# Hybrid decoder block: the residual's 128x128 transposes move from TensorE to VectorE blocks and SBUF-to-SBUF DMAs

## The chip, the cores and the metric

The kernel runs on one core of one Trainium2 chip. The metric is the device time of one execution in microseconds, the median of three runs. One execution was also taken by the hardware profiler; its trace is what the views below are read from.

## The reference, cut to what matters

The reference is one layer of a decoder: three head groups read one normed input, their outputs are joined and projected, a residual is added, and cross-attention into a memory follows. All is float32, 256 tokens, width 2048. The change touches the path from the first residual to the cross-attention's queries:

```python
y = concatenate([y_lru, y_ml, y_mo], axis=-1)     # (256, 2048)
x = x + y @ w_out[l]                              # the residual x1
hx = rms_norm(x, xa_norm_g[l])
hm = rms_norm(mem, mem_norm_g[l])
x = x + memory_cross_attention(hx, hm, xa_wq[l], xa_wkv[l], xa_wo[l])
return rms_norm(x, final_norm_g)
```

In memory_cross_attention the queries are `hx @ wq`, a product over the 2048 channels, so x1, which `y @ w_out` leaves with tokens on the partitions, is wanted with channels on the partitions.

## The kernel before, in words

**Weights.** All weight matrices are one stream of 172 chunks of up to 512 KB, taken in a fixed order of groups (GROUPS). For chunk i, `load(i)` issues one DMA on SP (L172) into one of 4 buffers `raw`; `split(i)` makes a rounded half on ScalarE (L197, `wh`) and the rest on VectorE (L148, `wl`), 6 buffers each; `mm(i)` multiplies on TensorE (L260 and L261 for groups with channels out, L282 to L284 for groups with tokens out). Activations are split in the same way into pairs of tiles (`a_x`, `a_y`, `a_m`, `a_h`).

**The loop.** One step of the main loop traces, in this order: the split of chunk i+4 and the load of chunk i+8; `mm(i)`; the work that a group's last chunk starts (`done`); and one call of `step()`. The order is written out by hand: every engine and SP's queue runs its instructions in the order in which the loop traces them. `step()` advances the first generator in a queue to its next yield; when a generator is at its end, the same call goes on with the next one. `urgent` puts a generator at the head of the queue, `bg` at its tail. `load(i+8)` waits until `split(i+4)` has freed its `raw` buffer, and `split(i+4)` until `mm(i-2)` has freed its `wh` and `wl`.

**The groups around the change.** out0 to out3 are the four quarters of `y @ w_out`, 8 chunks each; ck0 and ck2 (4 chunks each) make the memory's keys from `a_m`; cq0 and cq2 (4 each) make the queries from `a_h`; cv follows. In each step of out3 `stage_split("m", j)` also makes one pair `a_m`: two ScalarE (L232) and two VectorE instructions (L151). `a_m` j takes the buffer of `a_y` j, so it waits until out3's matmuls of step j have read that.

**The residual.** At the end of out group g, `x1_evac(a, g)` goes to the head of the queue. Its first part adds the accumulators to x (VectorE, two of 128x512) and sums squares on ScalarE, through a scratch tile `yt` of one buffer (L852). Its next two parts, one a step, each do four 128x128 transposes on TensorE into PSUM (L858) and split the result into a pair `a_h` (`split_pair`: L239 on ScalarE, L148 on VectorE). So x1_evac holds the head of the queue for the step of the group's end and two more; in the step after those it ends and the next generator goes on.

**Behind it in the queue** wait x1_load(2) and x1_load(3) (DMAs of x, L843), then mem_stats: eight steps that load a piece of the memory (L222), each squared two steps later on ScalarE (into `yt`) and summed on GpSimd (L402), two idle steps, and `stats("m")`: four tiny matmuls (L426) on the sum of the squares, a power on GpSimd (L359), two VectorE instructions that write a diagonal tile into `yt` (L430), and one step later a matmul that reads that `yt` (L433).

A tile that is asked for again (one buffer, same tag) waits until everything that was traced on the old one has run, also what was traced later. Tag w1 holds the memory's keys from ck0's end, w2 the queries from cq0's end; both are free from out0's end until then.

Of the kernel before, what the change touches and what calls it, by code (L numbers as in the profile page):

```python
# [105 lines left out]
def kernel(ctx: ExitStack, tc: tile.TileContext, xT, memT, x, mem, ws, vec_d, lw_d, fg_d, out):  # L106
    nc = tc.nc
    V, S, P, G = nc.vector, nc.scalar, nc.tensor, nc.gpsimd
# [18 lines left out]
    def ps():  # L127
        nps[0] += 1
        return psp.tile([128, 512], F32, tag="ps", name=f"ps{nps[0]}")

    def big(tag, *shape):
        n = 1
        for s in shape:
            n *= s
        t = wk.tile([128, 1556], F32, tag=f"w{tag}", name=f"w{tag}")
        v = t[:, :n]
        if len(shape) == 2:
            v = v.rearrange("p (a b) -> p a b", a=shape[0])
        elif len(shape) == 3:
            v = v.rearrange("p (a b c) -> p a b c", a=shape[0], b=shape[1])  # L140
        return v

    def small(name, *shape):
        t = sm.tile([128, *shape], F32, name=name, tag=name)
        return t

    def tt(out, a, b, op):
        V.tensor_tensor(out, a, b, op)  # L148
# [58 lines left out]
    def act_pair(which, j):  # L207

        a = acts.tile([128, 2, 2, 256], F32R, tag="y" if which in "ym" else "x", name=f"a_{which}{j}")
        act_all[which][j] = a  # L210
        act_hi[which][j], act_lo[which][j] = a[:, :, 0, :], a[:, :, 1, :]
        return act_hi[which][j], act_lo[which][j]
# [22 lines left out]
    def split_pair(which, j, src):  # L235

        h, l = act_pair(which, j)
        src = src.rearrange("p (a b) -> p a b", a=2)
        S.activation(h, src, AF.Copy)  # L239
        tt(l, src, h.bitcast(F32), OP.subtract)  # L240
# [70 lines left out]
    p = ps()  # L311
    for _ in range(WARM):
        P.matmul(p[:, :256], ones[:, :128], ones, start=True, stop=True)
    ident = cst.tile([128, 128], F32, name="ident")
# [522 lines left out]
    X1 = {}  # L837
# [9 lines left out]
    def x1_evac(a, g):  # L847
        t1 = X1[g]
        for t in range(2):
            tt(t1[:, t, :], a[t], t1[:, t, :], OP.add)  # L850
            junk = small("yt", 512)
            S.activation(junk, t1[:, t, :], AF.Square, accum_out=ssq1[:, t, g:g + 1])  # L852
        yield
        for j in range(2):
            p = ps()
            for kk in range(2):
                for t in range(2):
                    P.transpose(p[:, kk * 256 + t * 128:kk * 256 + t * 128 + 128],  # L858
                                t1[:, t, (2 * j + kk) * 128:(2 * j + kk) * 128 + 128], ident)
            split_pair("h", 2 * g + j, p)  # L860
            yield

    def x1_rstd():
# [130 lines left out]


    queue = deque()

    def bg(*gens):
        queue.extend(gens)
# [6 lines left out]

    def step(n=1):

        while queue and n > 0:
            try:  # L1010
                if next(queue[0]):
                    return
                n -= 1
            except StopIteration:
                queue.popleft()

    def drain():
        while queue:
            step()

    def idle(n):
# [18 lines left out]
    def done(name, a):  # L1040
# [17 lines left out]
        elif name[0] == "q":  # L1058
            urgent(qk_evac("q", 7, a, int(name[1])))
        elif name[0] == "k":  # L1060
            urgent(qk_evac("k", 5, a, int(name[1])))
            if name == "k2":
                bg(ml_norm())
        elif name == "v0":
            urgent(v_evac(a, 0))
        elif name == "v1":
            urgent(v_evac(a, 1))
            bg(mo_heads())
        elif name == "z0":
            urgent(gate_z(name, a))  # L1070
        elif name == "z1":
            urgent(gate_z(name, a))
            bg(ml_y(), mo_y(0, 1))
        elif name == "z2":
            urgent(gate_z(name, a))
            bg(mo_y(1, 3), x1_load(0), x1_load(1), x1_load(2), x1_load(3), mem_stats())
        elif name.startswith("out"):
            g = int(name[3])
            urgent(x1_evac(a, g))
            if g == 3:  # L1080
                bg(x1_rstd())
        elif name.startswith("ck"):
            urgent(ck_evac(a, int(name[2])))
        elif name.startswith("cq"):
            urgent(cq_evac(a, int(name[2])))
        elif name == "cv":
            C["acc"] = a
# [12 lines left out]
    for i in range(NS):  # L1100
        while nsx < 8 and nsx <= i + 2:
            stage_split("x", "mix_g", nsx)
            nsx += 1
        while nsp <= min(i + SPLIT_AHEAD, max(i + 2, 2 * i - 2)):
            split(nsp)
            nsp += 1
            while nl < nsp + RAW_BUFS:
                load(nl)
                nl += 1
        mm(i)  # L1110
        if i == 0:
            late_consts()
        if 2 <= i < 6:
            xrow_load(i - 2)
        if i == 6:
            nc.sync.dma_start(lw, lw_d)
        if 6 <= i < 10:
            xrow_square(i - 6)
        g, j, kc = CHUNKS[i][:3]
        if GROUPS[g][0] == "out3":  # L1120
            stage_split("m", "mem_g", j)
        if (j + 1) * kc == NK:
            done(GROUPS[g][0], acc.pop(g))
        step()
    drain()
    cv_out(C["acc"])
    fg_load((1, 9))
# [67 lines left out]
```

## Time and profile before

| | us |
|---|---|
| median of 3 runs (521.16 to 522.33) | 522.2 |
| the profiled execution | 521.88 |
| its span, first to last instruction | 520.2 |
| TensorE busy (98% of the span) | 507.9 |
| VectorE busy (65%) | 338.0 |
| ScalarE busy (56%) | 292.8 |
| GpSimd busy (11%) | 54.8 |

The profiled execution's time and its span differ by 1.7 us, which lie outside the profiled instructions. PE is TensorE, PEld its weight loads, DVE VectorE, ACT ScalarE, POOL GpSimd, SP SyncE; SPq is SP's queue, which issues the DMAs. Matmuls are pipelined: one that is 0.39 us long may be followed by the next after 0.23 us, so what a matmul takes of the path is the distance from start to start. The granted clock was 1.00 in all stretches from 318 to 482 us.

### The profile page before, as it was taken

To read this page: it belongs to the slowest core of one execution; us is meant where nothing else is said; L and a number is where in the kernel's file an instruction comes from. 1 tells how busy PE (TensorE), PEld (TensorE's weight loads), DVE (VectorE), ACT (ScalarE), POOL (GpSimd) and SP (SyncE) were. 2 spreads that over 40 slices of the span, in tenths; PEclk is the share of its full clock that TensorE was granted. 3 is DMA by queue.
4 is the path that set the end of the run, shared out by engine and by line. 5 is a ranking of instruction groups with operands and counts; after the bars stand their busy time and mean duration, and the time that the engine had idled before them with its cause. 6 is when DMAs were issued, how large, how long until landed. Compare 5 with 4: busy or idle time off the path is not lost.

```text
span 520.2 us, 7578 instructions
## 1 busy us (share of the span) xinstructions
PE 507.9 (98%) x2814; PEld 448.8 (86%) x2814; DVE 338.0 (65%) x531; ACT 292.8 (56%) x476; POOL 54.8 (11%) x70
## 2 busy tenths in 40 slices
PE   8999999999999999999999999999999999999993
PEld 6999889998988888889988888888888888888883
DVE  5958848895397656548645466654658749637574
ACT  5775477678544333353545755543649467546353
POOL 2800001000132100002000000000132003000000
PEclk9999999999999999999999999999999999999998
DMA  8995635467446544435843465478575527734704
GB/s 274 360 412 180 187 120 167 139 221 230 160 160 178 186 161 163 151 92 183 271 155 121 137 209 179 164 272 325 188 264 174 194 66 259 237 128 129 234 3 161
DMA packets 31077, 98.74 MB, mean 190 GB/s; under 512 B 3520, under 2 KB 3904, under 8 KB 31040
## 3 DMA queue, kind: packets, MB, share of 16 engines
q1 hardware_dynamic: 30896, 98.25, 56.9%
q8 instruction: 22, 0.36, 0.3%
q14 instruction: 15, 0.12, 0.1%
q10 hardware_dynamic: 144, 0.01, 0.0%
HBM read 96.15 MB, written 2.10 MB: 189 GB/s over the span
## 4 chain that ended last, share of the span: by engine, by line
PE 85%; issue 6%; POOL 3%; DVE 3%; DMA 1%; ACT 1%; SPq 1%; POOLq 0%; ACTq 0%; DVEq 0%
PE acc_out L284 5%; PE acc_out L282 5%; PE acc_out L283 5%; PE acc_q L260 4%; PE acc_k L260 4%; PE acc_z L284 4%; PE acc_z L282 4%; PE acc_z L283 4%; PE acc_cq L260 3%; PE acc_lz L260 3%; PE acc_q L261 2%; PE acc_k L261 2%; PE acc_o L283 2%; PE acc_o L282 2%; PE acc_o L284 2%
## 5 line engine op out<-in xcount | busy, mean ns | idle before, releaser
L148 DVE TENSOR_TENSOR wl<-raw,wh 128x1024 fp32r<-128x1024 f32 (+3 forms) x166 | 199.6, 1212 | 111.7 <-ACT wh L197 109.3
L197 ACT ACTIVATE wh<-raw 128x1024 fp32r<-128x1024 f32 (+2 forms) x162 | 161.8, 1013 | 44.5 <-DMA raw<-ws 14.8
L282 PE MATMUL acc_out<-wh,a_y 128*128 128x512 f32 x128 | 50.8, 397 | 0.0
L284 PE MATMUL acc_out<-wh,a_y 128*128 128x512 f32 x128 | 49.9, 390 | 0.0
L283 PE MATMUL acc_out<-wl,a_y 128*128 128x512 f32 x128 | 49.8, 389 | 0.0
L282 PE MATMUL acc_z<-wh,a_x 128*128 128x512 f32 x96 | 39.6, 412 | 0.0
L284 PE MATMUL acc_z<-wh,a_x 128*128 128x512 f32 x96 | 37.6, 391 | 0.0
L283 PE MATMUL acc_z<-wl,a_x 128*128 128x512 f32 x96 | 37.5, 390 | 0.0
L260 PE MATMUL acc_k<-a_x,wh 128*128 128x512 f32 x96 | 34.4, 401 | 0.0
L260 PE MATMUL acc_q<-a_x,wh 128*128 128x512 f32 x96 | 34.1, 398 | 0.0
L451 POOL TENSOR_TENSOR w<-ev,rrow 128x512 f32<-128x512 f32 x11 | 17.5, 1589 | 153.6 <-DVE ev L148 153.6
L284 PEld LDWEIGHTS acc_out<-wh,a_y 128*128 128x128 f32 x128 | 24.0, 188 | 5.2
L283 PEld LDWEIGHTS acc_out<-wl,a_y 128*128 128x128 f32 x128 | 24.1, 188 | 4.7
L282 PEld LDWEIGHTS acc_out<-wh,a_y 128*128 128x128 f32 x128 | 24.1, 188 | 4.6
L261 PE MATMUL acc_k<-a_x,wl 128*128 128x256 f32 x96 | 26.9, 280 | 0.0
L261 PE MATMUL acc_q<-a_x,wl 128*128 128x256 f32 x96 | 26.8, 280 | 0.0
L402 POOL TENSOR_TENSOR mask<-mask,yt 128x512 f32<-128x512 f32 x7 | 10.3, 1473 | 147.1 <-ACT yt L401 147.1
L260 PE MATMUL acc_lz<-a_x,wh 128*128 128x512 f32 x64 | 23.3, 406 | 0.0
L260 PE MATMUL acc_ck<-a_m,wh 128*128 128x512 f32 x64 | 23.1, 403 | 0.0
L260 PE MATMUL acc_cq<-a_h,wh 128*128 128x512 f32 x64 | 22.7, 399 | 0.0
L283 PE MATMUL acc_o<-wl,a_x 128*128 128x392 f32 (+1 forms) x64 | 21.6, 338 | 0.0
L282 PE MATMUL acc_o<-wh,a_x 128*128 128x392 f32 (+1 forms) x64 | 21.6, 337 | 0.0
(302 smaller groups left out, 1187.4 us busy)
## 6 DMA issues: line engine op xcount, KB each, us to landing
raw<-ws SPq DMA_DIRECT2D x138, 512.0 KB, 4.1
raw<-ws SPq DMA_DIRECT2D x24, 384.0 KB, 3.1
w<-x SPq DMA_DIRECT2D x8, 512.0 KB, 6.5
raw<-ws SPq DMA_DIRECT2D x8, 392.0 KB, 3.1
w<-memT SPq DMA_DIRECT2D x8, 256.0 KB, 6.1
out<-xg SPq DMA_DIRECT2D x8, 256.0 KB, 3.0
w<-xT SPq DMA_DIRECT2D x7, 256.0 KB, 6.7
raw<-ws SPq DMA_DIRECT2D x4, 256.0 KB, 5.0
```

What stands on the lines that cost most here:

```text
L148: V.tensor_tensor(out, a, b, op)
L197: S.activation(h[:, :kc * n], r[:, :kc * n], AF.Copy)
L260: P.matmul(a[m], h[:, sl], both, start=first, stop=False, skip_group_check=True)
L261: P.matmul(a[m][:, :256], l[:, sl], xh, start=False, stop=last, skip_group_check=True)
L282: P.matmul(o, xh[:, sl], mh, start=first, stop=False)
L283: P.matmul(o, xh[:, sl], ml, start=False, stop=False)
L284: P.matmul(o, xl[:, sl], mh, start=False, stop=last)
L402: G.tensor_tensor(sq[which], sq[which], q, OP.add)
L451: G.tensor_tensor(dst, e, rb(which), OP.mult)
```

## The change: what it does, and the diff

x1_evac ends after its first part and puts a new generator, x1_turn(g), in a list `side`. Every call of `step()` now first advances each generator of that list once, and then the queue as before. x1_turn transposes the 128x1024 residual of a group in 32x32 blocks with one VectorE instruction into a tile of tag w1 (`tmp`), and then moves the blocks to their places in a tile of tag w2 (`xT1`) with 16 DMAs, four a step: each takes 32 partitions, 8 pieces of 32 floats each (128 bytes) a partition, 32 KB in all. After one more step the two pairs `a_h` are split from xT1, one a step. The loads, splits and matmuls of the weights are the same.

```diff
@@ x1_evac(a, g)
             S.activation(junk, t1[:, t, :], AF.Square, accum_out=ssq1[:, t, g:g + 1])
         yield
+        side.append(x1_turn(g))
+
+    def x1_turn(g):
+        tmp, xT1 = big(1, 8, 128), big(2, 8, 128)
+        V.transpose(tmp.rearrange("p (c t) k -> p c t k", t=2), X1[g].rearrange("p t (c k) -> p c t k", k=128))
+        for i in range(4):
+            for j in range(4):
+                nc.sync.dma_start(xT1[32 * j:32 * j + 32, :, 32 * i:32 * i + 32],
+                                  tmp[32 * i:32 * i + 32, :, 32 * j:32 * j + 32])
+            yield
+        yield
         for j in range(2):
-            p = ps()
-            for kk in range(2):
-                for t in range(2):
-                    P.transpose(p[:, kk * 256 + t * 128:kk * 256 + t * 128 + 128],
-                                t1[:, t, (2 * j + kk) * 128:(2 * j + kk) * 128 + 128], ident)
-            split_pair("h", 2 * g + j, p)
+            split_pair("h", 2 * g + j, xT1[:, 4 * j:4 * j + 4].rearrange("p a c -> p (a c)"))
             yield
@@ the queue
     queue = deque()
+    side = []
     def step(n=1):
+        for g in list(side):
+            if next(g, True):
+                side.remove(g)
         while queue and n > 0:
...
     def drain():
-        while queue:
+        while queue or side:
             step()
```

## Rows read from the trace of the kernel before

**Rows 1.** The page, part 1: busy us by engine, share of the span, instructions.
```profile
PE 507.9 (98%) x2814; PEld 448.8 (86%) x2814; DVE 338.0 (65%) x531; ACT 292.8 (56%) x476; POOL 54.8 (11%) x70
```

**Rows 2.** TensorE in order of time, out1 (start us, duration us, what).
```profile
344.95 0.39 PE L284 MATMUL acc_out<-wh,a_y 128*128 128x512 f32 x1
345.18 0.60 PE L858 MATMUL ps<-ident,w 128*128 128x128 f32 x4
345.54 0.47 PE L282 MATMUL acc_out<-wh,a_y 128*128 128x512 f32 x1
...
346.07 0.39 PE L284 MATMUL acc_out<-wh,a_y 128*128 128x512 f32 x1
```

**Rows 3.** TensorE in order of time, ck0: a block of transposes that waited.
```profile
413.81 0.91 PE L858 MATMUL ps<-ident,w 128*128 128x128 f32 x4
414.48 0.47 PE L260 MATMUL acc_ck<-a_m,wh 128*128 128x512 f32 x1
...
414.90 0.40 PE L260 MATMUL acc_ck<-a_m,wh 128*128 128x512 f32 x1
```

**Rows 4.** ScalarE, VectorE in order of time; in brackets idle time and its releaser.
```profile
421.27 0.63 ACT L852 ACTIVATE yt<-w 128x512 f32<-128x512 f32 x1 [9.16 <-PE ps L433]
423.73 1.22 DVE L148 TENSOR_TENSOR wl<-raw,wh 128x1024 fp32r<-128x1024 f32 x1 [9.61 <-ACT wh L197]
```

**Rows 5.** TensorE in order of time, ck2's first chunk.
```profile
423.45 0.40 PE L260 MATMUL acc_ck<-a_m,wh 128*128 128x512 f32 x1
...
423.80 0.46 PE L260 MATMUL acc_ck<-a_m,wh 128*128 128x512 f32 x1
425.01 0.39 PE L261 MATMUL acc_ck<-a_m,wl 128*128 128x256 f32 x1 [0.76 <-DVE wl L148]
425.23 0.39 PE L260 MATMUL acc_ck<-a_m,wh 128*128 128x512 f32 x1
```

**Rows 6.** Groups of instructions by line (count, busy us, mean ns, idle before).
```profile
L858 PE MATMUL ps<-ident,w 128*128 128x128 f32 x32 | 5.0, 274 | 0.1
L148 DVE TENSOR_TENSOR w<-w,w 128x1024 f32<-128x1024 f32 x2 | 2.4, 1219 | 0.0
L148 DVE TENSOR_TENSOR w<-acc_out,w 128x512 f32<-128x512 f32 x8 | 5.1, 683 | 3.0 <-DMA w<-x 3.0
L402 POOL TENSOR_TENSOR mask<-mask,yt 128x512 f32<-128x512 f32 x7 | 10.3, 1473 | 147.1 <-ACT yt L401 147.1
```

**Rows 7.** In order of time: out1's fifth chunk split, another's split, its first matmul.
```profile
345.68 1.23 DVE L148 TENSOR_TENSOR wl<-raw,wh 128x1024 fp32r<-128x1024 f32 x1 [1.90 <-ACT wh L197]
346.31 1.05 ACT L197 ACTIVATE wh<-raw 128x1024 fp32r<-128x1024 f32 x1
354.27 0.39 PE L282 MATMUL acc_out<-wh,a_y 128*128 128x512 f32 x1
```

**Rows 8.** SP's queue in order of time: issue of DMAs (start us, duration us).
```profile
352.21 0.43 SPq L843 DMA_DIRECT2D w<-x  x1
352.97 0.33 SPq L172 DMA_DIRECT2D raw<-ws  x1
```

**Rows 9.** DMAs, whole run: packets, MB, share; then issues, KB each, us to landing.
```profile
q1 hardware_dynamic: 30896, 98.25, 56.9%
w<-memT SPq DMA_DIRECT2D x8, 256.0 KB, 6.1
vec<-vec ACTq DMA_DIRECT2D x1, 8.0 KB, 2.2
```

**Rows 10.** DMA issues from 383 to 385 us: KB each, us to landing.
```profile
w<-memT SPq DMA_DIRECT2D x1, 256.0 KB, 3.8
```

**Rows 11.** DMA queues from 0 to 12 us: packets, MB, share of 16 engines.
```profile
q10 hardware_dynamic: 144, 0.01, 0.8%
```

**Rows 12.** VectorE in order of time: the diagonal tile of the memory's statistics.
```profile
410.51 0.48 DVE L430 TENSOR_SCALAR yt<-ident,rstd_m 128x128 f32<-128x128 f32 x2 [0.82 <-POOL rstd_m L359]
```

**Rows 13.** Out1: busy us of PE, PEld, DVE, ACT, POOL; clock, DMA share, GB/s.
```profile
342.00:364.00 22.00, 22.00 (x102) 18.24 (x101) 11.19 (x12) 11.21 (x15) 0.00 (x0) 1.00 0.83 299
```

## The prediction, made before the changed kernel was run

> **What bounds the kernel now.** I read the page first: TensorE is busy for 98% of the span [rows 1], so what is taken off it counts, and what is put before it counts as soon as it waits. Then TensorE in order of time: in out1 a matmul follows the last after 0.23 us, across the blocks of transposes too [rows 2]; a step of 12 matmuls takes 2.72 us, a group of eight 21.8. Then the other engines beside it. VectorE and ScalarE are each busy 11.2 of 22 us in out1 [rows 13], and work ahead: the split of out1's fifth chunk ends at 346.9 us, its first matmul starts at 354.27 [rows 7]. This lead of 7.4 us hides whatever delays them by less. Last the waits: the one long one near the change is ScalarE's 9.16 us before the squares of out3's end [rows 4]. Those squares want the tile `yt`, which the memory's statistics hold until L433's matmul, traced three steps later. VectorE idles 9.61 us with it, the lead is gone, and TensorE waits in ck2 [rows 5].
>
> **What it removes from TensorE.** 32 transposes in 8 blocks of four. Without the block in out1 the third matmul after it would start at 345.18 + 2 x 0.225 = 345.63 instead of 346.07: 0.44 us [rows 2]. Seven of the eight blocks are like it. The eighth waited: the matmul at 414.90 would have come one pair (0.35 us, 423.45 to 423.80 [rows 5]) after 413.81, at 414.16: 0.74 us [rows 3]. Together 7 x 0.44 + 0.74 = 3.8 us. Bounds: nothing, were TensorE waiting there anyway, and 5.0 us, all their busy time [rows 6]; TensorE has no gap beside the blocks, so I take 3.8. The rows show 0.11 us of the path for a transpose. The Trainium skill (VectorE: DVE Perf Modes, The three transpose paths) gives 390 ns for one on TensorE, and its rules for kernel authors keep 128x128 transposes there wherever a PSUM destination will do; by that figure 12.5 us would go and the sum would end 8.7 us lower, but the distance in the trace decides.
>
> **What moves in the queue.** x1_evac now holds the queue for one step instead of three, so all behind it comes two steps sooner for each group. The memory's statistics, which ended three steps after out3, get L426 after out3's first step and L433 after its second. `yt` is free again at out3's end, and the 9.16 us wait is gone. What TensorE gets back: the pair at 425.23 would have started at 423.80 + 0.35 = 424.15, so 1.1 us [rows 5]. What is late next there: nothing that I see, the lead then being whole. So far 3.8 + 1.1 = 4.9 us.
>
> **What it adds.** VectorE gets four block transposes. The trace has none; the same 1024 columns with two sources take 1.22 us [rows 6]. I take 1.2, between half of that for one source and twice for two passes; 4.8 us on an engine half idle hides in the lead. Without that cover each would cost up to 1.2.
> SP gets 16 DMAs a group. Issues take 0.33 and 0.43 us [rows 8]; I take 0.43, the one of more pieces, and as far end 2.2, the smallest DMA's whole time to landing [rows 9]. Four, a weight load and one more load are 2.48 of a step's 2.72 us: the queue holds, barely. The first four wait for the block transpose, and behind them on SP wait the loads of weights, of x and of the memory.
> On the DMA engines a DMA is 256 pieces of 128 bytes and 16 semaphore writes, 17 packets an engine. 64-byte pieces took 0.8% x 16 x 12 us / 144 = 10.7 ns [rows 11], an average packet of 3.2 KB 56.9% x 16 x 520.2 us / 30896 = 153 ns [rows 9]; on the line between them 128 bytes take 14 ns. That is 0.2 us a DMA and 3.8 a group, with the far end at 2.6 and 42 us. The engines were 0.83 busy in out1 [rows 13], so 3.7 us are free: just enough.
> Waits: ScalarE waits for all 16 DMAs before a pair; behind it are weight splits, under the lead. GpSimd's first write of the memory's keys waits for out3's last DMAs, traced a step later; nothing behind it is near its due time.
>
> **What the move puts before TensorE.** The memory's pieces are now loaded in out1 and early out2, each behind four of the new issues, and ScalarE squares each two steps after its load. I follow it from the end of out0, with a split 1.05 on ScalarE and 1.23 on VectorE [rows 7], an accumulator's addition 0.68 and a square's sum 1.47 [rows 6], a square or half pair 0.63 [rows 4], landing 6.1 us [rows 9].
> 1. VectorE ends the additions and two splits at 5.5 and the block transpose at 6.7. SP issues four DMAs (8.4), x (8.8), weights (9.2), four DMAs (10.9), the memory's first piece: landed 17.0. ScalarE is there at about 9 and waits.
> 2. Squares end at 17.6, 20.1 and 22.6, paced by SP's 2.48 us a step. A split, a pair and out1's additions and squares follow: 27.9, that is 6.1 after out1's end, where without delay it is 2.2.
> 3. Counted from out1's end: the sixth piece goes out behind a split that ended at 8.4 and lands at 14.9; the seventh and eighth have the next block transpose and 4 and 8 DMAs before them, land at 19.1 and 21.6, and the last square ends at 22.3.
> 4. Then three splits, two pairs, out2's additions and squares (30.3), another split, one `a_m` (VectorE 33.5), the power and the diagonal tile (0.82 + 0.48 [rows 12]): 35.0.
> TensorE comes to L433 at 21.8 + 2 x 2.72 + 0.4 = 27.6 and runs in order, so it waits 7.4 us. Bounds: 0, if ScalarE kept its lead, and 12 at twice the DMA price. The lead, which hid such lateness for splits, doesn't help here, since L433 stands at the head of TensorE's own queue. After the wait the lead is whole and nothing is given back.
>
> **The sum.** 521.88 - 4.9 + 7.4 = 524.4 us for the profiled execution, which is 0.3 us below the median of 522.2; so 524.7.
>
> **Rivals.**
> A, the forecast: TensorE waits at L433, 524.7. For it: the order of the loop and the landing of 6.1. Against: five hops add up, so an error of 0.5 us in a hop is 2.5 in the sum. Its own range is 522 to 528.
> B, faster: the memory's pieces land sooner. The piece loaded between 383 and 385 us took 3.8 us, with no x load beside it [rows 10]. With 3.8 in all hops the same walk ends 4.7 us earlier, the wait is 2.7, and the time 521.88 - 4.9 + 2.7 + 0.3 = 520.0; with no wait 517.3. It decides from a landing of 4.9 us down, where the wait is under 4.9. Against it: x and the memory are now loaded within the same few steps, beside 83% busy DMA engines.
> C, slower by more: SP is the bound. Above (2.72 - 0.76) / 4 = 0.49 us an issue, SP falls behind by 4 x (c - 0.49) a step. At 0.86, double my price, the hops of A grow by 6.8 us in out1 and 3.4 in out2: 524.7 + 10 = 535. For it: nothing like these DMAs is in the trace; against: the issues of 0.33 and 0.43. The Trainium skill (DMA: Bandwidth & Descriptors, Rules for kernel authors) speaks for it: small transfers should be merged, those under 64 KB being mostly overhead, and these are 32 KB each. If each held the queue for its whole 2.2 us [rows 9], a group would need 16 x 2.2 + 4.8 = 40 us of SP for 21.8 of TensorE, some 70 us more in all: I give that 2 in 100.
> D, the change saves nothing beyond what it costs: the wait at L433 is near 4.9, 522.2.
>
> **How the numbers follow.** A measurement tells 0.3%, 1.6 us, from no change. A has 0.50 (slower 0.44, within 0.06), B 0.30 (faster 0.27, within 0.03), C 0.11 (slower), D 0.09 (within 0.08, faster 0.01). So faster 0.28, same 0.17, slower 0.55. The time is A's, 524.7. The range reaches from no more than a short wait at L433 (518) to C's near part (531); left out are B's best end, C's far end and worse.
>
> **What would show it.** After the change there is no transposing matmul of the residual; out0 to out3 start every 0.23 us; SP shows runs of four issues; ScalarE waits for the memory's DMAs in out1 and out2; TensorE shows one gap of some 7 us at L433, after out3's second step, released by VectorE's diagonal tile; the waits at out3's end and in ck2 are gone. No gap at L433 is B, gaps before splits all through out1 to out3 are C. Wrong altogether would be TensorE's distance across a group's end unchanged.

## The result, and the profile after

The changed kernel takes 537.62 us (median of 4 runs, 536.42 to 538.72), the kernel before 521.89 beside it: a ratio of 1.0306, 95% interval 1.0291 to 1.0322. It is slower, as forecast, but by 15.7 us and not by 2.5, and it lies outside the range of 518 to 531. The profiled execution took 538.72 us, with a span of 537.0; of before it was 521.88 and 520.2.

The page first. Part 1, TensorE; then two rows of part 2, the span in 40 slices: its busy tenths and the clock granted to it.

```profile
PE 510.8 (95%) x2782; PEld 448.8 (84%) x2782; DVE 340.3 (63%) x535; ACT 293.0 (55%) x476; POOL 54.8 (10%) x70
...
PE   8999999999999999999999999999864999999993
...
PEclk9999999999999999999999999999986999999998
```

TensorE has 32 instructions fewer than in [rows 1], those of the transposes, and yet is busy for 2.9 us longer; its share fell from 98 to 95%. The loss sits in slices 29 to 31, which are the second half of out2 and most of out3, and the clock falls in the same place. The windows of the stages give it in numbers: out1, out2, out3, then ck with cq, then the rest (columns as in [rows 13]).

```profile
343.10:364.80 21.70, 21.70 (x97) 17.98 (x96) 8.27 (x8) 7.53 (x11) 0.00 (x0) 1.00 0.81 234
364.80:392.10 27.30, 23.04 (x98) 17.59 (x96) 13.60 (x13) 13.39 (x20) 8.05 (x6) 1.00 0.72 213
392.10:430.00 37.90, 27.82 (x103) 21.83 (x104) 25.00 (x34) 20.55 (x34) 3.94 (x4) 0.82 0.66 179
430.00:475.20 45.20, 45.20 (x258) 39.23 (x257) 32.23 (x58) 27.13 (x57) 4.39 (x3) 1.00 0.66 200
475.20:537.00 61.80, 53.13 (x270) 44.86 (x268) 36.59 (x65) 30.64 (x60) 1.10 (x2) 0.96 0.40 135
```

The same stages of the kernel before:

```profile
342.50:365.20 22.70, 22.70 (x106) 18.81 (x105) 12.38 (x13) 11.21 (x15) 0.00 (x0) 1.00 0.82 298
365.20:387.80 22.60, 22.60 (x105) 18.75 (x104) 13.00 (x12) 13.28 (x19) 7.24 (x5) 1.00 0.64 211
387.80:411.00 23.20, 23.20 (x110) 19.26 (x109) 20.08 (x30) 17.20 (x30) 4.58 (x5) 1.00 0.64 204
411.00:458.80 47.80, 46.95 (x268) 40.42 (x267) 30.82 (x55) 26.46 (x56) 4.55 (x3) 1.00 0.58 192
458.80:520.20 61.40, 53.15 (x270) 44.86 (x268) 36.71 (x65) 30.66 (x60) 1.10 (x2) 0.97 0.37 121
```

Stage by stage, by the first number behind each window: out1 gains 1.0 us and ck with cq 2.6, as forecast. Out2 loses 4.7: TensorE, which had no gap there, is now idle for 27.30 - 23.04 = 4.26 us. Out3 loses 14.7: 37.90 - 27.82 = 10.1 us idle, and 4.6 us more of busy time, in which its matmuls take longer at a lower clock. With 0.6 us up to the end of out0 and 0.4 at the end that makes the 16.8 us between the spans. The waits behind the idle time (TensorE, 364 to 418 us: engine, tile, line, releaser, us in all, times, longest):

```profile
PE ps L433 <- DVE yt L430: 7.5, 1, 7.5
PE acc_out L283 <- DVE wl L148: 2.8, 3, 1.0
PE acc_out L282 <- ACT wh L197: 2.5, 2, 1.6
PE ps L426 <- POOL mask L404: 1.6, 1, 1.6
```

L433 is the wait of the forecast. The two rows of L282 and L283 are not: there TensorE comes to a chunk of weights before its split is done, so the lead of [rows 7] is used up. What ate it is seen on SP's queue in order of time:

```profile
355.57 4.17 SPq L863 DMA_DIRECT2D w<-w  x4
359.83 0.54 SPq L222 DMA_DIRECT2D w<-memT  x1
360.48 0.38 SPq L172 DMA_DIRECT2D raw<-ws  x1
360.90 2.83 SPq L863 DMA_DIRECT2D w<-w  x4
363.78 0.60 SPq L222 DMA_DIRECT2D w<-memT  x1
...
364.90 2.79 SPq L863 DMA_DIRECT2D w<-w  x4
367.73 0.60 SPq L222 DMA_DIRECT2D w<-memT  x1
```

L863 is a block DMA, L222 a piece of the memory, L172 a load of weights. Four block DMAs take 2.8 us of SP, and pieces go out every 3.95 us (359.83, 363.78, 367.73) where TensorE wants a step every 2.72. Not all of that is the issues: SP also waits for DMAs to land (between 340 and 460 us: us in all, times, longest; then the load of weights issued at 349.13, with its us to landing):

```profile
SPq L863 <- DMA raw<-ws: 2.8, 4, 1.7
SPq L863 <- DMA w<-x: 0.9, 1, 0.9
...
raw<-ws SPq DMA_DIRECT2D x1, 512.0 KB, 8.7
```

All five of these waits end when the DMA that SP issued eight DMAs earlier lands: the program has eight semaphores for SP's DMAs and takes them in turn, so SP never has more than eight under way. In the kernel before none of its DMAs waited for a landing between 340 and 460 us. Here one such wait, 0.92 us, lies in front of the 4.17 us row and one of 1.68 within it; the second ends at 357.82, when the load of 349.13 lands. In the two steps behind, 0.34 and 0.29 of the 3.95 us are such a wait. One DMA and the block transpose by themselves:

```profile
w<-w SPq DMA_DIRECT2D x64, 32.0 KB, 3.6
w<-memT SPq DMA_DIRECT2D x8, 256.0 KB, 3.8
...
q1 hardware_dynamic: 48304, 100.35, 58.2%
```

```profile
L860 DVE STREAM_TRANSPOSE w<-w x4: 1230/1236/1239, 348.6 to 438.6; 128x1024 f32<-128x1024 f32 x4
```

Last L433 itself, on TensorE in order of time:

```profile
399.36 0.63 PE L282 MATMUL acc_out<-wh,a_y 128*128 128x512 f32 x1
399.79 0.63 PE L283 MATMUL acc_out<-wl,a_y 128*128 128x512 f32 x1
...
410.53 1.19 PE L433 MATMUL ps<-yt,ones 128*128 128x256 f32 x2 [7.54 <-DVE yt L430]
...
412.80 0.63 PE L282 MATMUL acc_out<-wh,a_y 128*128 128x512 f32 x1
413.23 0.63 PE L283 MATMUL acc_out<-wl,a_y 128*128 128x512 f32 x1
...
416.83 0.39 PE L284 MATMUL acc_out<-wh,a_y 128*128 128x512 f32 x1
417.06 0.39 PE L282 MATMUL acc_out<-wh,a_y 128*128 128x512 f32 x1
```

After the wait a matmul follows the last every 0.43 us, and only from about 416.4 on every 0.23. It was so before the wait too, from 399 to 402.3 us, behind the waits of 1.58 and 0.98 us for a split and of 1.56 at L426. The windows say why: a granted clock of 0.65 and 0.54, close to the lower of the two levels (1.2 of 2.4 GHz).

```profile
398.40:411.20 12.80, 5.26 (x17) 3.89 (x16) 7.65 (x13) 7.03 (x13) 0.71 (x1) 0.65 0.50 167
411.20:416.40 5.20, 5.20 (x15) 4.05 (x14) 3.37 (x5) 1.33 (x2) 0.00 (x0) 0.54 0.40 120
```

### The profile page after: what moved, and what is told of

The parts are those of the page before. It is cut to its first block, busy times and chain, and to the rows that moved or that the text cites. A ratio compares the mean times of both kernels' runs of the same rounds, so it can differ in the third digit from the quotient of the medians.

```text
span 537.0 us, 7617 instructions
## 1 busy us (share of the span) xinstructions
PE 510.8 (95%) x2782; PEld 448.8 (84%) x2782; DVE 340.3 (63%) x535; ACT 293.0 (55%) x476; POOL 54.8 (10%) x70
## 3 DMA queue, kind: packets, MB, share of 16 engines
q1 hardware_dynamic: 48304, 100.35, 58.2%
## 4 chain that ended last, share of the span: by engine, by line
PE 81%; issue 6%; DMA 4%; POOL 3%; SPq 2%; DVE 2%; ACT 1%; ACTq 0%; POOLq 0%
PE acc_q L260 4%; PE acc_k L260 4%; PE acc_z L284 4%; PE acc_z L282 4%; PE acc_z L283 4%; PE acc_out L282 4%; PE acc_out L283 4%; PE acc_out L284 4%; PE acc_cq L260 3%; PE acc_ck L260 3%; PE acc_lz L260 3%; PE acc_k L261 2%; PE acc_o L283 2%; PE acc_q L261 2%; PE acc_o L282 2%
## 5 line engine op out<-in xcount | busy, mean ns | idle before, releaser
L282 PE MATMUL acc_out<-wh,a_y 128*128 128x512 f32 x128 | 52.6, 411 | 2.5 <-ACT wh L197 2.5
L283 PE MATMUL acc_out<-wl,a_y 128*128 128x512 f32 x128 | 51.6, 403 | 2.8 <-DVE wl L148 2.8
L284 PE MATMUL acc_out<-wh,a_y 128*128 128x512 f32 x128 | 51.3, 401 | 0.0
L282 PE MATMUL acc_z<-wh,a_x 128*128 128x512 f32 x96 | 39.6, 412 | 0.0
L283 PE MATMUL acc_z<-wl,a_x 128*128 128x512 f32 x96 | 37.5, 390 | 0.0
L283 PEld LDWEIGHTS acc_out<-wl,a_y 128*128 128x128 f32 x128 | 25.0, 196 | 9.0 <-DVE wl L148 3.9
L282 PEld LDWEIGHTS acc_out<-wh,a_y 128*128 128x128 f32 x128 | 25.0, 195 | 8.8 <-ACT wh L197 3.6
L284 PEld LDWEIGHTS acc_out<-wh,a_y 128*128 128x128 f32 x128 | 24.9, 194 | 5.4
L260 PE MATMUL acc_ck<-a_m,wh 128*128 128x512 f32 x64 | 22.6, 399 | 0.0
L283 PE MATMUL acc_o<-wl,a_x 128*128 128x392 f32 (+1 forms) x64 | 21.6, 338 | 0.0
L282 PE MATMUL acc_o<-wh,a_x 128*128 128x392 f32 (+1 forms) x64 | 21.6, 337 | 0.0
```

The costliest lines, as they stand in the source:

```text
L260: P.matmul(a[m], h[:, sl], both, start=first, stop=False, skip_group_check=True)
L282: P.matmul(o, xh[:, sl], mh, start=first, stop=False)
L283: P.matmul(o, xh[:, sl], ml, start=False, stop=False)
L284: P.matmul(o, xl[:, sl], mh, start=False, stop=last)
```

## The experiments

Theory: what costs the time is the place of the block DMAs in SP's queue. An issue takes 0.6 us there and not 0.43, so weight loads and memory pieces behind them come late, and ScalarE, VectorE and TensorE after them. Rivals: the short packets on the DMA engines; the new order of work; the block transpose; the splits' own wait for the last block DMA. Each time below stands against the kernel before in the same series (521.7 to 522.1 us). e4_few, e15_few_tiny, e6_vec, e11_nowait and e14_vec_late leave the blocks in their partitions and e3_tiny moves a quarter of them, so these six measure a time and not a result.

| kernel | us | against before | ratio, 95% |
|---|---|---|---|
| changed kernel | 537.62 | +15.7 | 1.0291 to 1.0322 |
| e1_hold | 532.74 | +10.7 | 1.0187 to 1.0233 |
| e2_pe | 524.23 | +2.2 | 1.0025 to 1.0051 |
| e3_tiny | 533.76 | +11.8 | 1.0198 to 1.0239 |
| e4_few | 529.01 | +7.0 | 1.0111 to 1.0146 |
| e15_few_tiny | 525.29 | +3.6 | 1.0054 to 1.0081 |
| e6_vec | 522.32 | +0.6 | 1.0005 to 1.0024 |
| e11_nowait | 536.18 | +14.5 | 1.0237 to 1.0294 |
| e8_three | 545.04 | +23.4 | 1.0407 to 1.0480 |
| e12_two | 533.52 | +11.9 | 1.0174 to 1.0259 |
| e5b_pool3 | 535.87 | +13.8 | 1.0248 to 1.0281 |
| e7_act | 535.04 | +12.9 | 1.0222 to 1.0288 |
| e9_late | 533.98 | +12.3 | 1.0217 to 1.0264 |
| e10_pool_late | 535.12 | +13.0 | 1.0221 to 1.0270 |
| e13_two_late | 532.32 | +10.7 | 1.0181 to 1.0219 |
| e14_vec_late | 517.47 | -4.2 | 0.9898 to 0.9927 |
| b2_pe_late | 520.75 | -1.4 | 0.9959 to 0.9981 |
| b1_owntile | 520.47 | -1.3 | 0.9960 to 0.9983 |

**Are the block DMAs the cause at all?** e2_pe keeps the new order but not the DMAs; e6_vec keeps the VectorE transpose too.

```diff
 # e2_pe, x1_turn
-        V.transpose(tmp..., X1[g]...)          # and the 16 DMAs
+        for i in range(5):
+            yield
         for j in range(2):
+            p = ps()                           # four P.transpose, as before
+            split_pair("h", 2 * g + j, p)
 # e6_vec, x1_turn
         for i in range(4):
-            for j in range(4):
-                nc.sync.dma_start(xT1[...], tmp[...])
             yield
-            split_pair("h", 2 * g + j, xT1[...])
+            split_pair("h", 2 * g + j, tmp[...])
```

> Changed kernel with its new order of work (side list, one-step hold, memory pieces two steps earlier), but the residual's transposes stay on TensorE, from the row tile into PSUM, and the splits read PSUM; no VectorE transpose and no block DMA. Issue theory: with the block DMAs gone SP has at most 1.4 us of issues a step, the splits keep their lead, and only the order's own effects stay (the 1.1 us of the waits at the end of out3 and in ck2 gained, something at L433 lost): 520 to 523 us. Packet theory: the same 520 to 523. Queue-move theory: the loss stays, 530 to 538.

> Changed kernel without any block DMA: VectorE's transposes stay, and the splits read their tile, so that the blocks stay in their partitions and the residual is not transposed across them. SP-queue theory: the kernel with TensorE's transposes in this order (524.2) less their 3.8 us: 519 to 522 us. If VectorE's transpose of 1.2 us or the order itself were the price: 526 to 536.

524.23 and 522.32 (1.2 and 0.3 us over the intervals named): without the DMAs the loss is nearly gone, so neither the order nor VectorE is by itself its cause. What is left in both is a wait at L433 of 2.1 and 3.1 us. Of the 15.7 us the 64 DMAs cost 15.1.

**Issues or packets?** Two by two: all or a quarter of the issues, all or a quarter of the packets.

```diff
 # e3_tiny
-  nc.sync.dma_start(xT1[32*j:32*j+32, :, 32*i:32*i+32], tmp[32*i:32*i+32, :, 32*j:32*j+32])
+  nc.sync.dma_start(xT1[32*j:32*j+32, 0:2, 32*i:32*i+32], tmp[32*i:32*i+32, 0:2, 32*j:32*j+32])
 # e4_few: one a step, over all partitions
+  nc.sync.dma_start(xT1[:, :, 32*i:32*i+32], tmp[:, :, 32*i:32*i+32])
 # e15_few_tiny
+  nc.sync.dma_start(xT1[:, 0:2, 32*i:32*i+32], tmp[:, 0:2, 32*i:32*i+32])
```

> Changed kernel with its 64 block DMAs, each of which moves 2 of the 8 blocks of 32 words of a partition instead of all 8 (so 64 packets of 128 bytes a DMA and not 256); the splits read those two for every column, so the transposed residual is wrong in its other columns. Issue theory with a price per DMA: each issue stays at 0.6 us and the time at 534 to 539 us. Issue theory with a price per packet or row described: the issue falls towards 0.35 us, and the time to 517 to 524. Packet theory (engines): 517 to 524 with the issue unchanged at 0.6 us.

> Changed kernel with 4 block DMAs a group instead of 16, one a step, each over all 128 partitions with 8 pieces of 128 bytes (1024 packets a DMA: as many packets and bytes in all as in the changed kernel, a quarter of the issues); the blocks stay in their partitions, so the residual is not transposed across them. Issue theory with a price per DMA: SP's step falls to 0.6 + 0.4 + a memory piece, about 1.5 us, and the time to 516 to 521 us. Packet theory, on the engines or at the issue: 532 to 538.

> Changed kernel with a quarter of the issues and a quarter of the packets: 4 block DMAs a group over 128 partitions, each with 2 of the 8 pieces of a partition; the splits read those two for every column, the blocks stay in their partitions. If what the block DMAs cost is the sum of their issues on SP and of their packets: 64 issues with a quarter of the packets gave +11.4 us over the kernel without block DMAs, 16 issues with all of them +6.7 and all of both +15.3, so the sum leaves 2.8 us for this one: 523.5 to 527. If the first DMA's wait for VectorE on SP's queue, which all four have in common, were the main price: 528 to 533.

Against before: +15.7 with all of both, +11.8 with a quarter of the packets, +7.0 with a quarter of the issues, +3.6 with a quarter of both, +0.6 with none. Three quarters of the issues are worth 15.7 - 7.0 = 8.7 or 11.8 - 3.6 = 8.2 us, three quarters of the packets 15.7 - 11.8 = 3.9 or 7.0 - 3.6 = 3.4. The two add up, as the last expectation had it (523.5 to 527). So for e4_few both theories had missed: neither is the whole price, the issues are some 70% of it. What an issue costs includes its place among the eight DMAs under way (between 340 and 460 us SP waits for landings for 3.7 us in the changed kernel, 1.9 in e3_tiny, 2.0 in e15_few_tiny and not at all in e4_few); these runs do not separate that from the 0.6 us. The issue is a price per DMA: e3_tiny came 0.2 us under the interval for that, and with 64 packets a DMA four of them still hold SP for 2.5 us, here without a wait among them:

```profile
358.17 2.52 SPq L863 DMA_DIRECT2D w<-w  x4
```

Where the packets act is seen on SP in e4_few, with 1024 packets a DMA. The block DMA itself (L862) takes the same 0.6 us, but the memory piece behind it is held at its issue for 3.02 and 2.27 us, where the median of the kernel before is 0.43 (longest 1.10), and e15_few_tiny, with 256 packets a DMA, has at most 1.12:

```profile
353.37 0.61 SPq L862 DMA_DIRECT2D w<-w  x1
354.08 3.02 SPq L222 DMA_DIRECT2D w<-memT  x1
...
357.96 0.61 SPq L862 DMA_DIRECT2D w<-w  x1
358.62 2.27 SPq L222 DMA_DIRECT2D w<-memT  x1
```

The Trainium skill (DMA: Bandwidth & Descriptors, Rules for kernel authors) wants small transfers merged. The runs agree: the same packets in a quarter of the DMAs take 8.7 us less.

**Who waits: what stands behind the issues, or the splits that read the result?** In e11_nowait the DMAs stay, and no split waits for them.

```diff
-            split_pair("h", 2 * g + j, xT1[:, 4 * j:4 * j + 4]...)
+            split_pair("h", 2 * g + j, tmp[:, 4 * j:4 * j + 4]...)
```

> Changed kernel with all its block DMAs, but the splits read VectorE's tile and not the tile that the DMAs fill, so that no split waits for a block DMA; the residual is then not transposed across the blocks of partitions. Queue theory (weight loads and memory pieces late behind the issues): nearly all of the loss stays, 533 to 538 us, with the wait at L433 still 7 us. Landing theory (the splits wait for the last block DMA, and ScalarE behind them): most of the loss goes, 522 to 528 us.

536.18, within the queue theory's interval. ScalarE's waits up to 418 us show whose lateness it is, the memory pieces':

```profile
ACT yt L401 <- DMA w<-memT: 13.6, 5, 5.2
...
ACT mask L398 <- DMA w<-memT: 8.7, 1, 8.7
```

TensorE waits 5.0 us at L433 there, 7 expected. DMAs that no split waits for cost nearly as much (14.5 of 15.7 us) as those that are waited for, by their place in the queue.

**Can the DMAs be put elsewhere?** In time: e1_hold holds the queue three steps as before, so that no memory piece stands among them; e8_three and e12_two deal out three and two a step.

```diff
 # e1_hold, x1_evac
         side.append(x1_turn(g))
+        yield
+        yield
 # e8_three, x1_turn (n = 4 * i + j; no idle step before the splits)
+            if n % 3 == 2 or n == 15:
+                yield
 # e12_two, x1_turn (both splits in the step after the last DMA)
+            if n % (2 if g < 3 else 4) == (1 if g < 3 else 3):
+                yield
```

> Changed kernel, with the queue held for two more steps after a group's evacuation, so that the memory pieces are issued in the same steps as before the change and not among the block DMAs. Issue theory (SP's queue is the bound: a block DMA occupies it about 0.62 us, so 4 of them, a weight load and a memory piece with its follow-up come to about 3.9 us of a 2.72 us step; without the piece about 2.9): most of the delay goes, the splits keep their lead, the 7.5 us wait at L433 goes too, and TensorE keeps its clock: 517 to 523 us. Packet theory (the 128-byte pieces of the block DMAs hold up the DMA engines and with them the weight loads): no gain from the order, 532 to 538. Queue-move theory (the memory norm's work moved to earlier steps is to blame, not the DMAs): back near the kernel before, 518 to 522.

> Changed kernel with the 16 block DMAs of a group dealt out three a step over six steps instead of four a step over four; the splits follow one step later. SP-queue theory: an SP step is 3 x 0.63 + 0.4 + 0.55 = 2.8 us where a step of TensorE is 2.72, so the queue just about holds while it lasts two steps longer: 525 to 532 us. Packet theory: the packets are the same, 532 to 538. If only the latency from the first to the last block DMA counted, it would be slower: 538 to 541.

> Changed kernel with the block DMAs of the first three groups dealt out two a step over eight steps, the fourth group's four a step as before; both splits of a group follow one step after its last DMA. Queue theory by the issue price: an SP step is 2 x 0.63 + 0.4 + 0.6 = 2.3 us, less than the 2.72 of TensorE, so the loads keep their place: 524 to 531 us. Latency theory (each issue ahead of a memory piece lengthens the round from a freed weight buffer over SP, the piece's landing, ScalarE's square and split back to VectorE, whatever SP's load is): the more steps have issues in them the worse, 538 to 548 us, with a wait at L433 above 8 us.

e8_three and e12_two fall in none of their intervals; e1_hold (532.74) misses the issue theory's 517 to 523 and falls in the packet theory's 532 to 538. In e1_hold the pieces are out of the way, but weights and loads of x are still among the DMAs, and SP's step is 3.8 us (the next load of weights goes out at 361.20):

```profile
357.43 0.41 SPq L172 DMA_DIRECT2D raw<-ws  x1
357.90 2.56 SPq L865 DMA_DIRECT2D w<-w  x4
360.50 0.60 SPq L843 DMA_DIRECT2D w<-x  x1
```

The splits then wait for their DMAs, 9.65 us on ScalarE at 368.39, and the lead is gone all the same. e8_three (545.04) is the worst of all. Its last DMA goes out at 369.08, and the first split of the pair stands in ScalarE's order ahead of out1's squares and of the next weights:

```profile
374.71 0.63 ACT L239 ACTIVATE a_h<-w 128x512 fp32r<-128x512 f32 x1 [3.82 <-DMA w<-w]
376.76 0.63 ACT L852 ACTIVATE yt<-w 128x512 f32<-128x512 f32 x1 [1.42 <-DVE w L148]
```

TensorE waits 3.6 us at L282 behind it, and then 11.1 at L433. e12_two, which has the pair behind the group's end, comes to 533.52: below e8_three though its DMAs are spread over more steps, so the latency theory falls, but 2.5 us above the queue theory's interval. SP is not full in it, but it stands still: from 355.0 to 356.4 us it waits for the load of weights issued eight DMAs earlier (348.44) to land. Two of SP's waits from 340 to 460 us:

```profile
SPq L863 <- DVE w L860: 10.1, 4, 3.4
SPq L172 <- DMA raw<-ws: 3.7, 3, 1.5
```

So a step's issues may sum to less than 2.72 us and the queue still be late, by the landings; the queue theory's sum left them out. The first DMA of a group also waits on SP for the block transpose, 10.1 us in all, and each piece still goes out behind two issues. Which of these is what remains was not isolated.

On other queues: the first three groups' DMAs from GpSimd (with all four, e5_pool, the program deadlocks and has no time), or every second one from ScalarE.

```diff
 # e5b_pool3
-                nc.sync.dma_start(xT1[...
+                (nc.gpsimd if g < 3 else nc.sync).dma_start(xT1[...
 # e7_act
+                (nc.sync, nc.scalar)[j % 2].dma_start(xT1[...
```

> Changed kernel with the block DMAs of the first three groups issued from GpSimd's queue and not from SP's; the fourth group's stay on SP. Bytes, packets, steps and the VectorE transpose are the same. SP-queue theory (what costs the time is that weight loads and memory pieces stand behind 0.6 us issues on SP): SP's step is back to 1.4 us, and the kernel comes near the one without block DMAs (522.3): 521 to 526 us, with 3 us left at L433. Packet theory (the short packets hold the DMA engines, whoever issues them): 530 to 538. If GpSimd's issues are much dearer than SP's, its late square sums would show it at L426, and the time would be over 526.

> Changed kernel with every second block DMA issued from ScalarE's queue: two a step there, two on SP. SP-queue theory: SP's step is 2 x 0.63 + 0.4 + 0.6 = 2.3 us, under TensorE's 2.72, and ScalarE's step grows by 1.2 us to 3.0 to 3.4 us in 4 of 8 steps, so part of the loss moves to ScalarE: 526 to 534 us. Packet theory: 532 to 538.

535.87: the 521 to 526 of the theory, in so far as it spoke of SP's queue alone, is wrong. SP is free again, but GpSimd has an in-order queue too, an issue takes 0.58 us there, and the square sums stand among the DMAs:

```profile
386.06 2.31 POOL L863 DMA_DIRECT2D w<-w  x4
388.39 1.76 POOL L402 TENSOR_TENSOR mask<-mask,yt 128x512 f32<-128x512 f32 x1
390.09 2.30 POOL L863 DMA_DIRECT2D w<-w  x4
```

ScalarE waits 11.0 us for those sums, and L426 on TensorE 4.3. That is the sign of the expectation's last branch, late square sums at L426, but not its condition: an issue is no dearer on GpSimd than on SP. e7_act (535.04) is 1.0 us over the 526 to 534 expected: between 340 and 470 us ScalarE stands idle for 7.3 us before splits and 4.8 before a square because of its own issues; 3.5 us of that an issue waited for an earlier block DMA to land (348.93, landed at 357.32). So wherever the 16 issues went in these runs, something due stood behind them. The packet theory's intervals hold e5b_pool3 and e7_act too, as they hold e1_hold; what speaks against packets as the main price is the two by two above, not these runs.

**What is the wait at L433 worth?** In e9_late the diagonal has a tile of its own and L433 comes three steps later; the same edit on four other kernels and, without the three steps, on the kernel before.

```diff
-        d = small("yt", 512)[:, :256]...
+        d = small("dg", 256)...
         yield
+        if which == "m":                       # not in b1_owntile
+            yield from idle(3)
         p = ps()
         P.matmul(p[:, :256], ones[:, :128], d..., start=True, stop=True)
```

> Changed kernel with the statistics' diagonal in a tile of its own and the matmul of L433 three steps later, so that nothing waits for it at the head of TensorE's queue; the block DMAs stay. If the wait at L433 is a cost of its own (7.5 us, and with it the 2 to 3 us of lower clock behind it): 527 to 531 us. If SP's queue sets the pace of the splits anyway, so that the time lost at L433 is lost at the next splits instead: 533 to 538.

> The kernel that issues the first three groups' block DMAs from GpSimd's queue, with the statistics' diagonal in a tile of its own and the matmul of L433 three steps later. If SP's queue and the wait at L433 are the two prices: the kernel without block DMAs (522.3) less its own wait at L433 (3.1 us) and the lower clock behind it (0 to 2 us): 517 to 520.5 us, below the kernel before. Packet theory: 528 to 534.

> The kernel with two block DMAs a step, with the statistics' diagonal in a tile of its own and the matmul of L433 three steps later. Queue theory: 520 to 527 us. Latency theory: 534 to 540 us.

> Changed kernel without any block DMA (VectorE transposes within the blocks, the splits read its tile, so the blocks stay in their partitions), with the statistics' diagonal in a tile of its own and the matmul of L433 three steps later. It bounds what the change could give if its DMAs were free: the kernel without block DMAs (522.3) less its wait at L433 of 3.1 us: 518 to 520 us; 521 to 523 if that wait is hidden.

> TensorE's transposes in the changed kernel's order of work (524.2 us), with the statistics' diagonal in a tile of its own and the matmul of L433 three steps later; no VectorE transpose and no block DMA. If the wait at L433 (2.1 us there) is a cost of its own: 520 to 522.5 us. If it is hidden anyway: 523.5 to 525.

> Kernel before, with the statistics' diagonal in a tile of its own; nothing else is changed. The prediction's second term says that ScalarE's wait of 9.16 us at the end of out3 costs TensorE 1.1 us: 520.5 to 521.2 us against 521.9. If that wait is hidden by the lead of the splits: 521.5 to 522.3.

With the block DMAs the wait goes and little is won: 537.6 to 533.98 (e9_late, within the 533 to 538 of a wait that is lost elsewhere), 535.87 to 535.12 (e10_pool_late), 533.52 to 532.32 (e13_two_late, which misses both of its intervals). The splits are late anyway, and TensorE stops for them instead; in e9_late it still waits over 6 us for splits between 340 and 460 us. Without the DMAs it is worth more than its length: e2_pe to b2_pe_late is 3.5 us for a wait of 2.1 (520.75, as expected), e6_vec to e14_vec_late 4.9 for 3.1 (expected 518 to 520, measured 517.47). The window from 395 to 405 us of e6_vec and of e14_vec_late shows the rest, the granted clock:

```profile
395.00:405.00 10.00, 9.29 (x34) 7.53 (x35) 7.67 (x12) 4.67 (x8) 0.05 (x1) 0.83 0.45 148
```

```profile
395.00:405.00 10.00, 10.00 (x46) 8.26 (x45) 10.00 (x16) 7.21 (x13) 0.00 (x0) 1.00 0.61 190
```

e10_pool_late missed by 15 us, with e5b_pool3's reason. b1_owntile (520.47, 1.3 us faster than before) came as expected. It and b2_pe_late are faster than both kernels. e14_vec_late, 4.2 us under before, is what the change with L433 moved would give if its DMAs cost nothing; it leaves the blocks in their partitions, and no version that moves them by DMAs came below 532.3.

## Why the prediction was wrong

1. *3.8 us of transposes taken from TensorE*: about right. Between b2_pe_late and e14_vec_late, alike but for where the transposes are made, lie 3.3 us (2.9 if each is taken against the kernel before in its own series), 0.09 to 0.10 us of the path a transpose. So here the trace's distance held and not the 390 ns that the Trainium skill (VectorE: DVE Perf Modes, The three transpose paths) gives for bf16, which made it 12.5; these transposes are float32.
2. *1.1 us of the wait at out3's end*: right. The tile alone gave 1.3 (b1_owntile). In ck with cq two blocks of transposes (0.74 + 0.44) and the wait of [rows 5] make 2.3 of the 2.6 us gained.
3. *VectorE's transposes, 1.2 us each and hidden*: 1.236, and hidden (e6_vec).
4. *The issue on SP, 0.43 us, "the queue holds, barely"*: this is the step that failed. I took the price of [rows 8] from loads of 128 rows; the block DMA takes 0.61 (median of 64), and the loads beside it rise from 0.33 to 0.38 and from 0.43 to 0.60. A step is then 4 x 0.60 + 0.38 + 0.60, 0.3 us between them and 0.3 of waiting for a landing: 3.95 us for 2.72. That SP waits for landings had no term at all. The memory's first piece was to go out 10.9 us after out0's end (343.1) and went out at 16.7. Of these 5.8 us the two waits of 0.92 and 1.68 are 2.6, one block DMA whose issue was held for 1.51 us is 0.9, and what is left, 2.3, is the price of the issues. The text named the point itself: above 0.49 us SP is the bound. That was rival C, with 0.11, and its sign, gaps before splits, came in out2 and out3.
5. *The lead hides late splits; only L433 counts*: failed with it. By the walk the memory's first three squares end 17.6, 20.1 and 22.6 us after out0's end; they ended at 21.2, 24.8 and 29.0, so 3.6, 4.7 and 6.4 us later. SP's lag is not paid once but grows in each step with DMAs, and the weights' splits stand between the squares on ScalarE. The lead of 7.4 us was down to 1.0 at the split of out2's second chunk. TensorE then waited for splits, 4.3 us idle in out2 alone. C's own formula, 10 us for 0.43 us more, gives 4.7 for the 0.2 us measured, and 529.4: it too let only L433 count, and no landing.
6. *The wait at L433, 7.4 us*: measured 7.54, and that is chance. By the walk TensorE was to come there 27.6 us after out1's end, at 392.4, and the diagonal to be ready at 35.0, at 399.8. It came at 403.0, and L433 ran at 410.5. Both were 10.6 us late, so their distance stayed.
7. *"After the wait the lead is whole and nothing is given back"*: the clock was left out. Out3's busy time is 4.6 us longer. The clock had fallen ahead of L433 already, behind the waits for splits and at L426.
8. *Packets at 14 ns*: about right. The share of 16 engines rose from 56.9% of 520.2 to 58.2% of 537.0 us, 264.6 engine us for 17408 packets more: 15.2 ns, if the other packets took what they took before. That they fit beside 83% busy engines at no cost was not: they are worth 3.4 to 3.9 us for three quarters of them.
9. *Pieces land 6.1 us after their issue*: 3.8. Rival B's condition (under 4.9) was met and its gain did not come, because the delay lay before the issue and not behind it.

## What to carry to other kernels

Count every DMA that a step issues at the price of its own shape on its queue, and compare the sum with the step: a DMA is paid by whatever stands behind it in that in-order queue, whether or not anyone waits for it. Count the DMAs under way too: where a queue takes its semaphores in turn, a cheap DMA can have to wait for a slow load several places before it. A lead of some steps hides a delay that comes once, not one that comes in each step. And a wait of an engine at the head of its own queue should be costed with the clock behind it.

## What the runs showed of the hardware

- The issue of a block DMA holds SP for 0.60 to 0.61 us in the median, with 64, 256 or 1024 packets alike (e3_tiny, the changed kernel, e4_few; three of the changed kernel's 64 took 0.75 to 1.62), ScalarE's queue for 0.62 (e7_act) and GpSimd's for 0.58 (e5b_pool3); a weight load of 512 KB takes 0.33.
- With 1024 short packets a DMA (e4_few), the issue of the memory piece behind it was held for up to 3.02 us; with 256 (e15_few_tiny) for at most 1.12.
- A stop of 2.1 or 3.1 us of TensorE at L433 (e2_pe, e6_vec) left a granted clock of 0.83 in the window from 395 to 405 us, against 1.00 without the stop (b2_pe_late, e14_vec_late), and cost 1.4 to 1.8 us beyond its own length.
